# A hybrid decoder layer: other orders of the first two recurrence blocks, SSD rows turned by DMA with a new chunk order, and the FFN's first down rows and third weight rows asked for sooner

## The chip, the cores and the metric

The kernel runs on one core of one Trainium2 chip. The metric is the device time of one execution in microseconds. A core has five engines with a queue of instructions each: TensorE (PE, with its weight loads PEld), VectorE (DVE), ScalarE (ACT), GpSimd (POOL) and SyncE (SP, which issues most of the DMAs here). Each engine takes its own queue in order; engines wait for each other only through semaphores.

## The reference

One decoder layer over 2048 tokens of width 1024, in float32. The first half has two mixers side by side on the normalised rows: a state-space mixer (SSD, 8 heads of 64, chunks of 128 tokens) and an RWKV-7 recurrence (8 heads of 64). Their outputs, side by side, go through one matrix, are normalised and added to the input. The second half is a gated FFN of width 2816 with a causal convolution of 3 taps.

```python
def reference(x, ...):
    xn = _rms_norm(h, pre_mix_norm[l])
    p_ssd, p_rwkv = jnp.split((xn @ w_in[l]).astype(jnp.float32), [SSD_COLS], axis=-1)
    y_ssd = _ssd_mixer(p_ssd, ...)
    y_rwkv = _rwkv7_mixer(p_rwkv, ...)
    mix = jnp.concatenate([y_ssd, y_rwkv], axis=-1).astype(h.dtype) @ w_out[l]
    h = h + _rms_norm(mix, post_mix_norm[l])
    hn = _rms_norm(h, pre_ffn_norm[l])
    u = _causal_dwconv(hn @ ffn_w_up[l], ffn_conv_w[l], ffn_conv_b[l])
    gate, val = jnp.split(u, 2, axis=-1)
    f = (jax.nn.silu(gate) * val) @ ffn_w_down[l]
    h = h + _rms_norm(f, post_ffn_norm[l])
```

## The kernel before

Three phases follow each other on PE, and each begins before the one ahead of it has ended. A matmul operand is kept as two float16 numbers, a rounded one (hi) and the rest (lo), and a product is the sum of three passes over these.

**Phase R, the recurrence** (to about 1005 us): 16 blocks of 128 tokens. The order of the work is written out by hand in strings, one token for a step: FIRST for block 0, SECOND for block 1 (PE still finishes block 0 there), PLAN for those that follow. In FIRST the weights also come in: w.k loads one piece of them and splits it into hi and lo on ACT and DVE. f.d.k and f.conv.k are projections of the block, f.gram.k its Gram matrices gr, from which DVE makes G, which goes through DRAM and comes back as atl; f.chain.k is a quarter of a triangular solve on DVE, 8 steps of a multiplication and an addition on atl and xl. conv makes the convolution of two column groups of the SSD's input: its last part, on ACT, POOL and DVE, makes ca. In phase R's block 0 the order of ACT and DVE is the order of the code; later the framework schedules all engines but PE.

**Phase S, the SSD** (about 950 to 1436 us): 16 chunks of 128 tokens. S_PLAN is the order of one chunk n, of which a letter says which chunk a step serves: c this one, n the next, p the one before, q that of two before, s and t a pair of chunks; Z takes one gate projection (z, 6 matmuls) from a list. p.o.a.b is the product with the output weights, q.post.0 and q.post.1 finish the rows of a chunk: two norms (ACT squares into a spare view, POOL makes the reciprocal roots, DVE scales), the residual on POOL, then the rows xi, ready for the FFN, are turned by PE, four 128 x 128 blocks in each part, copied out of PSUM by ACT into hT (128 x 8 x 128, one buffer) and written to DRAM as HN. hT also serves as the spare view for the squares. S_TAIL is the order behind the last chunk, where F takes one product of the FFN.

**Phase F, the FFN** (from 1378 us): two halves of 1024 tokens, each with 22 rows f of up-products (u, seven of them a row, 12 matmuls each) and 11 pairs of down-products (d). The inner products of both use seven products in place of eight, so operands are sums of blocks made on POOL (us, L1355) and split into hi and lo on ACT (L1224) and DVE or POOL (L1229, L1231). Rows f = 0 and 1 run in code order, as one product per F of S_TAIL. From f = 2 on the steps go to Program: it knows what each reads and writes, gives each a due time from PE's order, and at each moment lets an engine take the ready step with the smallest due time less LEAD, a number for the kind of step ("V C0 C0" is a DVE step that writes C0 from C0).

SP issues the DMAs in the order of the code or of the scheduler, and an issue that waits holds those behind it. The steps of the change are in the class of phase R's blocks (load, conv, chain, from L392), the chunk's post (L1079) with its lines L1085 (square), L1087, L1088, L1093 (xi), L1098 (transposes ht), L1099 (hT), L1101 (HN), and the loop over f in phase F (L1771).

## Time and profile before

| what | value |
| --- | --- |
| time, median of 3 runs | 2658.02 us (2654.33 to 2658.92) |
| the profiled execution | 2655.3 us |
| its span, first to last instruction | 2653.5 us |
| mean granted clock of TensorE | 0.977 of full |
| busy: PE, DVE, ACT, POOL | 93%, 74%, 46%, 47% of the span |
| mean DMA rate | 117 GB/s |

The busy share is an average over stretches with different limits, so the table by stretch, further down, tells more. A line such as "L1098 PE MATMUL ht<-ident_s,xi" names the line of the kernel, the engine, the operation, and the tiles written and read; xN is a count. TensorE's clock has two levels, 2.4 and 1.2 GHz; a mean of 0.98 over a stretch says that it stood at the lower one for 4% of the time.

### The profile page before, as it was taken

How to read it: one execution, taken by the hardware profiler on the slowest of the kernel's cores; microseconds unless marked ns; L12 is line 12 of the kernel's file. 1: busy time of each engine (PE TensorE's matmuls, PEld its weight loads, DVE VectorE, ACT ScalarE, POOL GpSimd, SP SyncE). 2: the span in 40 equal slices, each digit the busy share in tenths (PEclk: the TensorE clock that was granted, in tenths of full speed). 3: DMA queues.
4: the chain of work that ended last, by engine and by line, in shares of the span. 5: the costliest groups of instructions: out<-in, count | busy, mean ns of one | idle time of the engine just before them, and what ended most of it. 6: DMA issues, size and time to landing. Idle time of an engine off the chain costs nothing. (4 is left out here: it accounts for less than half of the span.)

```text
span 2653.5 us, 53912 instructions
## 1 busy us (share of the span) xinstructions
PE 2454.5 (93%) x21324; PEld 1551.8 (58%) x21340; DVE 1951.9 (74%) x3655; ACT 1210.2 (46%) x2467; POOL 1258.0 (47%) x1324
## 2 busy tenths in 40 slices
PE   5889999899999888999998899999989999999998
PEld 4788888888888855555543344444434444444443
DVE  6777777777777765666668879999999836555557
ACT  6555556555555443444444554544453433223132
POOL 2344444444444352333456865867667623123135
PEclk8899999999999998999999999999999999999999
DMA  7233222232222253344355454444435543333243
GB/s 213 71 66 73 54 54 63 61 83 58 54 62 56 49 178 106 124 131 138 126 179 192 132 174 163 137 173 143 171 119 196 182 143 103 100 99 107 84 154 112
DMA packets 309341, 310.74 MB, mean 117 GB/s; under 512 B 168160, under 2 KB 213600, under 8 KB 305760
## 3 DMA queue, kind: packets, MB, share of 16 engines
q1 hardware_dynamic: 307792, 305.72, 38.2%
q8 instruction: 167, 2.74, 0.4%
q10 hardware_dynamic: 1296, 1.58, 0.2%
q14 instruction: 86, 0.70, 0.1%
HBM read 187.85 MB, written 110.99 MB: 113 GB/s over the span
## 5 line engine op out<-in xcount | busy, mean ns | idle before, releaser
L1383 PE MATMUL u<-b,w 128*128 128x512 f16 x3696 | 810.8, 382 | 18.1 <-DVE C L1401 7.1
L1383 PEld LDWEIGHTS <-w 128*128 128x128 f16 x3696 | 362.7, 98 | 462.6 <-issue 25.9
L294 PE MATMUL d<-xt,wr 128*128 128x129 f16 x5376 | 338.1, 225 | 17.8 <-DMA xt<-xh 15.5
L294 PEld LDWEIGHTS <-wr 128*128 128x128 f16 x5376 | 323.9, 101 | 31.8 <-ACT wr L257 15.5
L1619 PE MATMUL d<-dw,fa 128*128 128x512 f16 x1512 | 332.1, 379 | 4.8 <-DMA dw<-DW 2.5
L1619 PEld LDWEIGHTS <-fa 128*128 128x128 f16 x1596 | 156.2, 98 | 203.8 <-issue 15.5
L1401 DVE TENSOR_TENSOR C<-u,C 128x512 f32<-128x512 f32 x220 | 150.5, 685 | 160.6 <-PE u L1383 155.5
L294 PE MATMUL c<-xt,wc 128*128 128x131 f16 x3072 | 204.0, 227 | 21.7 <-ACT tv L434 10.6
L294 PEld LDWEIGHTS <-wc 128*128 128x128 f16 x3072 | 188.2, 100 | 36.0 <-issue 29.5
L1632 DVE TENSOR_TENSOR acc<-d,acc 128x512 f32<-128x512 f32 x212 | 140.1, 683 | 52.1 <-PE d L1619 51.2
L581 DVE TENSOR_TENSOR tmp<-atl,xl 128x60 f32<-128x60 f32 (+24 forms) x465 | 136.4, 293 | 48.4 <-DMA atl<-ATd 33.0
L1229 POOL TENSOR_TENSOR fa<-p,fa 128x512 f16<-128x512 f32 x100 | 142.7, 1441 | 41.5 <-ACT fa L1224 41.5
L1231 DVE SCALAR_TENSOR_TENSOR w<-us,w 128x512 f16<-128x512 f32 x132 | 143.1, 1094 | 24.7 <-ACT w L1224 23.1
L1436 DVE SCALAR_TENSOR_TENSOR p<-C,fpar,p 128x1024 f32<-128x1024 f32 x88 | 129.4, 1470 | 34.1 <-ACT p L1432 34.0
L457 DVE SCALAR_TENSOR_TENSOR ca<-rc,cw,ca 128x128 f32<-128x128 f32 x384 | 132.7, 391 | 21.8 <-POOL ca L452 21.5
L584 DVE TENSOR_TENSOR xl<-xl,tmp 128x60 f32<-128x60 f32 (+24 forms) x465 | 127.9, 275 | 11.2
L1397 ACT ACTIVATE C<-u 128x512 f32<-128x512 f32 x88 | 52.3, 594 | 176.4 <-PE u L1383 157.8
L1436 DVE SCALAR_TENSOR_TENSOR a<-C,fpar,a 128x1024 f32<-128x1024 f32 x88 | 125.6, 1427 | 4.1 <-ACT a L1432 2.3
L1355 POOL TENSOR_TENSOR us<-us,us 128x512 f32<-128x512 f32 x66 | 105.5, 1602 | 48.6 <-DVE w L1231 31.0
L1224 ACT ACTIVATE fa<-p 128x512 f16<-128x512 f32 x110 | 65.6, 624 | 131.0 <-DVE p L1449 118.1
L1224 ACT ACTIVATE w<-us 128x512 f16<-128x512 f32 x132 | 80.7, 623 | 86.5 <-POOL us L1355 51.1
L694 POOL TENSOR_TENSOR tS<-S,Pi 64x256 f32<-64x256 f32 x64 | 40.5, 633 | 167.5 <-DVE S L704 165.1
...
## 6 DMA issues: line engine op xcount, KB each, us to landing
...
```

The costliest lines, as they stand in the source:

```text
L294: nc.tensor.matmul(ps, w[:, a, kt, :], xt[:, b, kt, cols], start=n == 0, stop=n == 3 * KT - 1)
L457: V.scalar_tensor_tensor(out=acc[:, q], in0=raw[:, q, k:k + 128], scalar=cw[:, g + q, k:k + 1], in1=acc[:, q], op0=ALU.mult, op1=ALU.add)
L581: chain.tensor_tensor(out=tmp[:, :m, :n], in0=atl[:, j, j + 1:32].unsqueeze(1).to_broadcast([P, m, n]), in1=xl[:, :m, j:j + 1].to_broadcas ...
L584: chain.tensor_tensor(out=xl[:, :m, j + 1:32], in0=xl[:, :m, j + 1:32], in1=tmp[:, :m, :n], op=ALU.add)
L1224: S.activation(h, src, AF.Copy, **({} if scale is None else {"scale": scale}))
L1229: {"V": V, "G": G_}[engine].tensor_tensor(out=l, in0=src, in1=h, op=ALU.subtract)
L1231: V.scalar_tensor_tensor(out=l, in0=src, scalar=scale, in1=h, op0=ALU.mult, op1=ALU.subtract)
L1383: nc.tensor.matmul(bk[at], self.w[i][:, u, k, :], self.half.b[i][:, k, v, :], start=start and n == 0, stop=n == 11, skip_group_check=True)
L1401: op("V", .61, lambda: V.tensor_tensor(out=part(j, x), in0=bk[at], in1=part(*a), op=ALU.add), (("u", 4 * s + at), (*(c0, c1)[a[0]], a[1])) ...
L1436: V.scalar_tensor_tensor(out=o[j], in0=C[j][:, 2 - d:1026 - d], scalar=cw[:, g, 2 - d:3 - d], in1=o[j], op0=ALU.mult, op1=ALU.add)
L1619: nc.tensor.matmul(bk[s, t], pairs[m].a[i][:, u, t * P:t * P + P], pairs[m].w[n][0][:, v, :], start=new and m == 0 and u == v == 0, stop=m ...
L1632: V.tensor_tensor(out=acc[j][:, t], in0=bk[s, t], in1=acc[j][:, t], op=ALU.add)
```

## The change

Four things change. (1) The numbers of LEAD. (2) The orders FIRST and SECOND; for them conv can leave out its last part, which becomes a step of its own (taps), and the chain comes in eight parts of four steps and not four of eight. (3) In phase S the rows xi are turned by DMA: ACT rounds 512 columns to float16 (hl), DVE puts the rest in xi's own place, SP issues a DMA transpose of each (128 x 512 into 128 x 4 x 128, tile tu, one buffer), POOL adds the two into hT, and HN is written in two parts; PE and PSUM have no share in it. S_PLAN and S_TAIL have new orders. (4) The pools of the first down rows are opened, and the rows asked for, ahead of f = 1; the weights of f = 2 are asked for behind the fourth product of f = 1, and not behind the last.

```diff
@@ -59,7 +59,7 @@
 
-    LEAD = {"A C0 u": 21, "A p p": 20, "A w us": 23, "G cy C1": 36, "G fa fa": 6, "G rt r": -38, "Q r -": -4, "Q us -": -40, "V C0 C0": 27, "V C1 C0": 9, "V C1 C1": 1, "V a1 C1": 7, "V acc acc": -4, "V b b": 3, "V dw dw": 2, "V hx acc": 11, "V p C0": 8, "V p a1": -2, "V p p": 7, "V w p": 16, "V w us": -4}
+    LEAD = {"A C0 u": 16, "A fss acc": 9, "A p p": 12, "A w us": 20, "G cy C1": 40, "G rt r": -38, "Q r -": -4, "V C0 C0": 40, "V C1 C0": 10, "V C1 C1": 1, "V a1 C1": 9, "V acc acc": -4, "V b b": 3, "V hx acc": 9, "V p C0": 9, "V p a1": -2, "V p p": 7, "V w p": 12, "V w us": -4}
@@ -180,33 +180,40 @@
 S_RIGHT = (
-    "ident_s mhalf_s", "ssm pov por ss pnv pnr", "Y", "yr", "xi", "m", "gpost", "gpre2", "hT", "yt", "wo",
+    "ident_s mhalf_s", "ssm pov por ss pnv pnr", "Y", "yr", "xi", "m", "gpost", "gpre2", "hT", "hl", "tu", "yt", "wo",
 )
...
+F_SOON = (*(f"fa{i}0" for i in range(7)), "r0", "rt0")
 F_LATE = (
-    *(f"fa{i}{s}" for i in range(7) for s in range(2)), "acc0", "acc1", "acc2", "acc3", "acc4", "r0", "r1", "rt0", "rt1",
-    "dw", "fss fs2 fov for",
+    *(f"fa{i}1" for i in range(7)), "acc0", "acc1", "acc2", "acc3", "acc4", "r1", "rt1", "dw", "fss fs2 fov for",
 )
...
 S_PLAN = """
-c.begin c.decay.0 Z c.off p.norm c.keys Z c.decay.1 p.o.0.0 Z t.sums s.steps p.o.0.1 t.flip Z n.rows q.post.0 c.y c.state
-p.o.1.0 q.post.1 p.o.1.1
+c.begin Z c.off c.decay.0 Z p.norm Z Z c.decay.1 p.o.0.0 p.o.0.1 c.keys t.sums q.post.0 s.steps q.post.1 c.y t.flip
+n.rows p.o.1.0 c.state p.o.1.1
 """
 S_QUOTA = (3,) * 12 + (4,) * 3
 S_TAIL = """
-F F p.o.0.0 p.norm F p.o.0.1 p.o.1.0 p.o.1.1 F q.post.0 F q.post.1 F F F F F F p.post.0 F p.post.1
+F F F p.norm F F p.o.0.0 p.o.0.1 q.post.0 F p.o.1.0 F p.o.1.1 F q.post.1 F F p.post.0 F p.post.1 F
 """
 FIRST = """
...
+f.solve.1 f.chain.0 f.d.11 f.conv.0 f.chain.1 n.load f.conv.1.0 f.chain.2 f.taps.1 f.conv.2 f.d.12 f.chain.3 w.20
...
 """
 SECOND = """
...
+f.d.0 b.values f.d.1 f.d.2 f.d.3 f.d.4 f.low.0 b.own.0 f.low.1 f.scan f.d.5 f.keys f.d.6 f.d.7 f.d.8 b.merge.0 f.d.9
...
 """
@@ -436,7 +443,7 @@
-            def conv(self, g):
+            def conv(self, g, post=1):
 
                 i, q = self.it, g % 2
                 if q == 0:
@@ -444,9 +451,14 @@
                 dense(tc, self.pc[:, q, 0:131], WC[:, g], self.xt, slice(13, 144))
                 if q == 0:
                     return
-                g -= 1
-                raw = wk.tile([P, 2, 131], F32, name=f"rc_{i}_{g}", tag="raw", bufs=2)
-                S.activation(raw, self.pc[:, :, 0:131], AF.Copy)
+                self.rc = wk.tile([P, 2, 131], F32, name=f"rc_{i}_{g}", tag="raw", bufs=2)
+                S.activation(self.rc, self.pc[:, :, 0:131], AF.Copy)
+                if post:
+                    self.taps(g)
+
+            def taps(self, g):
+
+                i, raw, g = self.it, self.rc, g - 1
                 acc = wk.tile([P, 2, P], F32, name=f"ca_{i}_{g}", tag="ca", bufs=2)
                 for q in range(2):
                     G_.tensor_scalar(
@@ -570,20 +582,20 @@
                 if not begin:
-                    for k in range(4):
+                    for k in range(8):
                         self.chain(k)
 
             def chain(self, part):
                 atl, xl, tmp, XTd, it = self.atl, self.xl, self.tmp, self.XTd, self.it
                 chain = G_ if it == iters - 1 else V
-                for j in range(part * 8, min(part * 8 + 8, 31)):
+                for j in range(part * 4, min(part * 4 + 4, 31)):
                     n, m = 31 - j, j // 4 + 1
                     chain.tensor_tensor(
                         out=tmp[:, :m, :n], in0=atl[:, j, j + 1:32].unsqueeze(1).to_broadcast([P, m, n]),
                         in1=xl[:, :m, j:j + 1].to_broadcast([P, m, n]), op=ALU.mult)
                     chain.tensor_tensor(
                         out=xl[:, :m, j + 1:32], in0=xl[:, :m, j + 1:32], in1=tmp[:, :m, :n], op=ALU.add)
-                if part < 3:
+                if part < 7:
                     return
                 for q in range(4):
                     nc.sync.dma_start(
@@ -1080,8 +1092,8 @@
             if part == 0:
                 ss = wk.tile([P, 1], F32, name="ssm" + self.cf, tag="ssm")
-                self.hT = wk.tile([P, KT, P], F32, name="hT" + self.cf, tag="hT")
-                jk = self.hT.rearrange("p a b -> p (a b)")[:, 0:D // 2].bitcast(BF16)
+                self.hl = wk.tile([P, D], F16, name="hl" + self.cf, tag="hl")
+                jk = self.hl.bitcast(BF16)
                 S.activation(jk, m, AF.Square, accum_out=ss)
@@ -1092,13 +1104,17 @@
-            ps = (bank(f"ht{self.cf}{part}", "yb") if n >= N - 2 else bank(f"ht{self.cf}{part}", "o", 2))
-            for u in range(4):
-                kt = 4 * part + u
-                nc.tensor.transpose(ps[:, u, :], self.xin[:, kt * P:(kt + 1) * P], K.ident)
-            S.activation(self.hT[:, 4 * part:4 * part + 4, :], ps, AF.Copy)
-            if part == 1:
-                nc.sync.dma_start(HN[n // 8][:, :, P * (n % 8):P * (n % 8) + P], self.hT)
+            cs = slice(512 * part, 512 * part + 512)
+            hi = self.hl[:, cs]
+            S.activation(hi, self.xin[:, cs], AF.Copy)
+            lo = self.xin[:, 512 * part:512 * part + 256].bitcast(F16)
+            V.tensor_tensor(out=lo, in0=self.xin[:, cs], in1=hi, op=ALU.subtract)
+            tu = wk.tile([P, 2, 4, P], F16, name=f"tu{self.cf}{part}", tag="tu")
+            nc.sync.dma_start_transpose(tu[:, 0], hi)
+            nc.sync.dma_start_transpose(tu[:, 1], lo)
+            hT = wk.tile([P, 4, P], F32, name=f"hT{self.cf}{part}", tag="hT")
+            G_.tensor_tensor(out=hT, in0=tu[:, 0], in1=tu[:, 1], op=ALU.add)
+            nc.sync.dma_start(HN[n // 8][:, 4 * part:4 * part + 4, P * (n % 8):P * (n % 8) + P], hT)
 
@@ -1770,16 +1786,21 @@
             ready = []
             for f in range(NFF):
                 u = ups[n * NFF + f]
-                for _ in u.run():
+                if n == 0 and f == 1:
+                    ctx.enter_context(wk.open("left", F_SOON))
+                    pairs[0].load()
+                for k, _ in enumerate(u.run()):
                     if n == 0 and f < 2:
                         yield
+                        if f == 1 and k == 3:
+                            ups[2].weights()
                 if n == 0 and f < 2:
                     yield
                 if n == 0 and f == 1:
                     ctx.enter_context(wk.open("left", F_LATE))
                     ctx.enter_context(psp.open("left", [f"u{i}" for i in range(4, 8)]))
                     acc.extend(wk.tile([P, 4, Q], F32, name=f"acc{j}") for j in range(5))
-                if f < NFF - 1:
+                if f < NFF - 1 and (n, f) != (0, 1):
                     ups[n * NFF + f + 1].weights()
                 if fin and f < 4:
                     for j in (2 * f, 2 * f + 1):
@@ -1790,7 +1811,8 @@
                 if f % 2:
                     p = pairs[f // 2]
                     p.factors(ups[n * NFF + f - 1], u)
-                    p.load()
+                    if (n, f) != (0, 1):
+                        p.load()
                     ready.append(p)
                 if n == 0 and f == 1:
                     prog.on = True
```

SP, in the middle of the SSD, before; H, yr, xi and HN are rows written, the recurrence's output read, the input's rows read and the turned rows written, R and rows the decay's rows, xbc and xs the SSD's inputs:

```order
L1089 DMA H4_87<-m_4_19061 128x1024
L1062 DMA yr_6_19526<-YR3_76 128x8x128
L1064 DMA xi_5_19271<-in_x_dram 128x1024
L1101 DMA HN0_81<-hT_4_19369 1024x1x128
L869 DMA xbc_5_19662<-XC5_70 128x2048
L1089 DMA H5_88<-m_5_19273 128x1024
L929 DMA rows_4_19576<-pp_4_19570 16x384
L984 DMA R_8_19578<-rows_4_19576 3x8x128
L984 DMA R_9_19835<-rows_4_19576 3x8x128
L1062 DMA yr_7_19733<-YR3_76 128x8x128
L1064 DMA xi_6_19528<-in_x_dram 128x1024
L1101 DMA HN0_81<-hT_5_19581 1024x1x128
```

SP at the same place after:

```order
L1101 DMA H4_87<-m_4_19077 128x1024
L1113 DMA_TRANSPOSE tu_40_19343<-hl_4_19325 128x4x128
L1114 DMA_TRANSPOSE tu_40_19343<-xi_4_19075 128x4x128
L1117 DMA HN0_81<-hT_40_19346 128x4x128
L1113 DMA_TRANSPOSE tu_41_19411<-hl_4_19325 128x4x128
L1114 DMA_TRANSPOSE tu_41_19411<-xi_4_19075 128x4x128
L1074 DMA yr_6_19549<-YR3_76 128x8x128
L1076 DMA xi_5_19290<-in_x_dram 128x1024
L1117 DMA HN0_81<-hT_41_19414 128x4x128
L1101 DMA H5_88<-m_5_19292 128x1024
L1113 DMA_TRANSPOSE tu_50_19609<-hl_5_19591 128x4x128
L1114 DMA_TRANSPOSE tu_50_19609<-xi_5_19290 128x4x128
```

One HN becomes two, each behind a pair of transposes, and the transposes of the second half stand behind the first half's HN; L1113 reads the rounded half, L1114 the rest.

POOL in the middle of the SSD before, from the root of chunk 4's first norm (pov, por) to chunk 5's; m is the chunk's row, yt and ST the SSD's output and state, sgv and sgr the root for the norm of y:

```order
L1016 TENSOR_TENSOR yt_6_19204<-yt_6_19204,of_6_19233 128x512
L1088 TENSOR_TENSOR m_4_19061<-m_4_19061,xi_4_19059 128x1024
L1040 TENSOR_TENSOR ST1_17148<-ST0_17147,aend_6_19196 128x512
L272 TENSOR_SCALAR pnv_19380<-ssh_4_19378 128x1
L273 TENSOR_TENSOR pnr_19381<-pnv_19380,mhalf_s_18043 128x1
L272 TENSOR_SCALAR sgv_19406<-sgs_6_19402 128x2
L273 TENSOR_TENSOR sgr_19407<-sgv_19406,mhalf_s_18043 128x2
L272 TENSOR_SCALAR pov_19583<-ssm_5_19580 128x1
L273 TENSOR_TENSOR por_19584<-pov_19583,mhalf_s_18043 128x1
```

POOL at the same place after, from behind chunk 4's por:

```order
L1028 TENSOR_TENSOR yt_6_19222<-yt_6_19222,of_6_19241 128x512
L279 TENSOR_SCALAR pnv_19336<-ssh_4_19334 128x1
L280 TENSOR_TENSOR pnr_19337<-pnv_19336,mhalf_s_18049 128x1
L1052 TENSOR_TENSOR ST1_17148<-ST0_17147,aend_6_19214 128x512
L1116 TENSOR_TENSOR hT_40_19346<-tu_40_19343 128x512
L279 TENSOR_SCALAR sgv_19432<-sgs_6_19428 128x2
L280 TENSOR_TENSOR sgr_19433<-sgv_19432,mhalf_s_18049 128x2
L1116 TENSOR_TENSOR hT_41_19414<-tu_41_19411 128x512
L279 TENSOR_SCALAR pov_19593<-ssm_5_19590 128x1
L280 TENSOR_TENSOR por_19594<-pov_19593,mhalf_s_18049 128x1
```

Two additions (L1116) that read what the transposes wrote stand in the row now, one ahead of the y norm's root and one ahead of the next chunk's pov.

DVE in block 0 of the recurrence before, from the first half of G; wr and wc are weights split from wst, and xl and tmp the chain's tiles:

```order
L550 TENSOR_TENSOR G_0_268<-gr00_0_701,cst_195 128x512
L550 TENSOR_TENSOR G_0_268<-gr01_0_702,cst_195 128x512
L258 SCALAR_TENSOR_TENSOR wr_204<-wst13_713,gwr_237,wr_204 128x4x128 x2
L258 SCALAR_TENSOR_TENSOR wc_205<-wst14_719,gwr_237,wc_205 128x4x128 x2
L258 SCALAR_TENSOR_TENSOR wc_205<-wst15_725,gwr_237,wc_205 128x4x128 x2
L258 SCALAR_TENSOR_TENSOR wc_205<-wst16_731,gwr_237,wc_205 128x4x128 x2
L550 TENSOR_TENSOR G_0_268<-gr10_0_737,cst_195 128x512
L550 TENSOR_TENSOR G_0_268<-gr11_0_738,cst_195 128x512
L258 SCALAR_TENSOR_TENSOR wc_205<-wst17_763,gwr_237,wc_205 128x4x128 x2
L258 SCALAR_TENSOR_TENSOR wc_205<-wst18_819,gwr_237,wc_205 128x4x128 x2
L258 SCALAR_TENSOR_TENSOR wc_205<-wst19_825,gwr_237,wc_205 128x4x128 x2
L399 COPY xt_1_831<-xt_0_239 128x16x3
L581 TENSOR_TENSOR tmp_0_761<-atl_0_755,xl_0_760 128x31
```

DVE at the same place after:

```order
L562 TENSOR_TENSOR G_0_268<-gr00_0_707,cst_195 128x512
L562 TENSOR_TENSOR G_0_268<-gr01_0_708,cst_195 128x512
L265 SCALAR_TENSOR_TENSOR wc_205<-wst14_719,gwr_237,wc_205 128x4x128 x2
L265 SCALAR_TENSOR_TENSOR wc_205<-wst15_750,gwr_237,wc_205 128x4x128 x2
L562 TENSOR_TENSOR G_0_268<-gr10_0_756,cst_195 128x512
L562 TENSOR_TENSOR G_0_268<-gr11_0_757,cst_195 128x512
L265 SCALAR_TENSOR_TENSOR wc_205<-wst16_768,gwr_237,wc_205 128x4x128 x2
L265 SCALAR_TENSOR_TENSOR wc_205<-wst17_774,gwr_237,wc_205 128x4x128 x2
L265 SCALAR_TENSOR_TENSOR wc_205<-wst18_780,gwr_237,wc_205 128x4x128 x2
L265 SCALAR_TENSOR_TENSOR wc_205<-wst19_786,gwr_237,wc_205 128x4x128 x2
L593 TENSOR_TENSOR tmp_0_804<-atl_0_798,xl_0_803 128x31
```

Two rows of weight splits now stand between the halves of G where there were four, and four stand between the second half and the chain where there were three and a copy.

## Rows read from the trace of the kernel before

**Rows 1.** The page's busy times: us, share of the span and instructions of an engine.

```profile
PE 2454.5 (93%) x21324; PEld 1551.8 (58%) x21340; DVE 1951.9 (74%) x3655; ACT 1210.2 (46%) x2467; POOL 1258.0 (47%) x1324
```

**Rows 2.** The table by stretch: the window, its length, then busy us (and instructions) of PE, PEld, DVE, ACT and POOL, TensorE's granted clock, the DMA share and GB/s.

```profile
15.53:94.84 79.31, 50.45 (x587) 46.46 (x588) 60.47 (x140) 44.23 (x89) 19.89 (x20) 0.76 0.57 165
94.84:150.00 55.16, 53.30 (x896) 49.78 (x893) 37.46 (x108) 31.28 (x73) 20.95 (x27) 1.00 0.28 64
...
1039.10:1378.40 339.30, 319.22 (x1833) 183.28 (x1846) 226.60 (x405) 152.66 (x414) 133.80 (x149) 0.98 0.40 130
1378.40:1506.20 127.80, 110.92 (x489) 49.51 (x488) 101.30 (x96) 60.57 (x96) 94.56 (x76) 0.93 0.52 170
1506.20:1960.00 453.80, 446.85 (x2065) 201.49 (x2064) 415.60 (x447) 217.10 (x332) 316.97 (x241) 1.00 0.46 158
1960.00:2000.00 40.00, 29.89 (x115) 12.29 (x115) 37.05 (x44) 17.80 (x27) 14.66 (x12) 0.87 0.37 119
2000.00:2590.00 590.00, 584.96 (x2708) 264.38 (x2708) 361.99 (x417) 182.03 (x264) 209.92 (x231) 1.00 0.42 130
```

**Rows 3.** PE's waits for xi from 1039.1 to 1378.4 (us in total, times, longest), and the group of the transposes in the same stretch (busy us, mean ns, idle before).

```profile
PE ht L1098 <- DVE xi L1093: 11.8, 11, 3.1
...
L1098 PE MATMUL ht<-ident_s,xi 128*128 128x128 f32 x112 | 17.5, 279 | 12.0 <-DVE xi L1093 11.8
```

**Rows 4.** PE's timeline in one chunk: start, us, engine, line, operation; from one chunk's psc to the next's, with the second group of transposes and what follows it.

```profile
1084.43 0.61 PE L973 MATMUL psc<-xbc 128*128 128x128 f32 x4
...
1104.05 0.60 PE L1098 MATMUL ht<-ident_s,xi 128*128 128x128 f32 x4
1104.49 2.75 PE L1073 MATMUL o<-wo,Y 128*128 128x512 f16 x12
...
1107.52 0.61 PE L973 MATMUL psc<-xbc 128*128 128x128 f32 x4
```

**Rows 5.** The timelines of ACT, DVE and POOL in the same chunk: the square of the first norm, xi, and the y norm's root.

```profile
1087.81 1.06 ACT L1085 ACTIVATE hT<-m 128x1024 bf16<-128x1024 f32 x1 [1.06 <-DMA HN<-hT]
...
1096.98 1.28 DVE L1093 SCALAR_TENSOR_TENSOR xi<-m,pnr,gpre 128x1024 f32<-128x1024 f32 x1 [1.84 <-POOL pnr L273]
...
1104.02 0.22 POOL L272 TENSOR_SCALAR sgv<-sgs 128x2 f32<-128x2 f32 x1 [7.07 <-ACT sq L1030]
```

**Rows 6.** Durations of like operations on 512 columns: an ACT copy to float16 (minimum, median, maximum in ns), a DVE and a POOL operation on two tiles (busy us and mean ns, in the SSD), and the issue of HN.

```profile
L1224 ACT ACTIVATE w<-us x132: 611/623/633, 1342.0 to 1956.4; 128x512 f16<-128x512 f32 x132
...
L1056 DVE TENSOR_TENSOR Y<-pY,Y 128x512 f16<-128x512 f32 x14 | 9.5, 678 | 0.0
...
L1016 POOL TENSOR_TENSOR yt<-yt,of 128x512 f32<-128x512 f32 x14 | 18.3, 1306 | 0.0
...
L1101 SPq DMA_DIRECT2D HN<-hT x16: 518/561/571, 1059.4 to 1436.0; - x16
```

**Rows 7.** SP's timeline where a DMA that reads a transpose's result waits for it (XN behind xt; between them one other issue of two), the first transpose of the kernel, PE's wait for it, which ends with its first matmul at 15.53, and two small DMAs of the SSD of which the second reads what the first wrote (12 KB).

```profile
71.48 1.23 SPq L405 DMA_TRANSPOSE xt<-xin  x1
72.77 1.16 SPq L371 DMA_DIRECT2D wst<-in_w_c_dram  x2
74.57 0.54 SPq L406 DMA_DIRECT2D XN<-xt  x1
...
11.14 1.37 SPq L404 DMA_TRANSPOSE xt<-xh  x1
...
PE d L294 <- DMA xt<-xh: 15.5, 1, 15.5
...
1076.27 0.33 SPq L929 DMA_DIRECT2D rows<-pp  x1
1077.67 0.60 SPq L984 DMA_DIRECT2D R<-rows  x2
```

**Rows 8.** PE's waits from 1378.4 to 1506.5: us in total, times, longest.

```profile
PE ht L1098 <- DVE xi L1093: 5.6, 1, 5.6
PE u L1383 <- ACT w L1224: 5.1, 1, 5.1
PE u L1383 <- DVE C L1401: 2.4, 1, 2.4
PE ht L1098 <- ACT hT L1099: 2.3, 1, 2.3
```

**Rows 9.** The timelines of DVE, ACT and PE in block 0 of the recurrence; in brackets the idle time before and what ended it.

```profile
55.05 1.41 DVE L258 SCALAR_TENSOR_TENSOR wr<-wst,gwr,wr 128x512 f16<-128x512 f32 x2
56.37 4.06 DVE L258 SCALAR_TENSOR_TENSOR wc<-wst,gwr,wc 128x512 f16<-128x512 f32 x6
60.35 1.28 DVE L550 TENSOR_TENSOR G<-gr,cst 128x512 f32<-128x512 f32 x2
...
69.25 0.19 DVE L581 TENSOR_TENSOR tmp<-atl,xl 128x31 f32<-128x31 f32 x1 [3.07 <-DMA atl<-ATd]
...
80.64 0.42 ACT L461 ACTIVATE ct<-ca 128x256 f32<-128x256 f32 x1 [11.12 <-DVE ca L457]
...
83.12 2.80 PE L294 MATMUL c<-xt,wc 128*128 128x131 f16 x24 [10.62 <-ACT tv L434]
```

**Rows 10.** PE's two largest waits after 1506.5: us in total, times, longest.

```profile
PE d L1619 <- DVE dwx L1583: 6.0, 3, 3.5
PE u L1383 <- ACT C L1397: 4.9, 1, 4.9
```

More of the change, by code (lines that the diff above doesn't have):

```diff
@@ L202 @@
 S_TAIL = """
-F F p.o.0.0 p.norm F p.o.0.1 p.o.1.0 p.o.1.1 F q.post.0 F q.post.1 F F F F F F p.post.0 F p.post.1
+F F F p.norm F F p.o.0.0 p.o.0.1 q.post.0 F p.o.1.0 F p.o.1.1 F q.post.1 F F p.post.0 F p.post.1 F
 """
 FIRST = """
-w.0 w.1 w.2 w.3 f.d.0 w.4 w.5 l. f.d.1 f.d.2 f.low.0 f.d.3 w.6 f.low.1 f.d.4 f.d.5 w.7 w.8 f.keys f.scan w.9 w.10 f.norm f.d.6 w.11 f.d.7 f.d.8 f.d.9 f.receptance w.12 f.gram.0 w.13 w.14 w.15 w.16 f.gram.1 f.solve.1 w.17 f.d.10 f.conv.0 w.18 w.19 n.load f.chain.0 f.chain.1 f.conv.1 f.chain.2 w.20 f.d.11 f.d.12 f.d.13 w.21 f.conv.2 f.transposed.0 f.conv.3 f.conv.4 f.conv.5 f.transposed.1 f.conv.6 f.chain.3 f.conv.7
+w.0 w.1 l. w.2 w.3 w.4 w.5 f.d.0 f.d.1 f.low.0 f.d.2 f.d.3 f.d.4 w.6 f.low.1 w.7 f.d.5 f.scan w.8 f.keys w.9 w.10
+f.norm f.d.6 f.d.7 w.11 w.12 f.d.8 f.d.9 f.receptance w.13 f.gram.0 w.14 f.d.10 w.15 f.gram.1 w.16 w.17 w.18 w.19
+f.solve.1 f.chain.0 f.d.11 f.conv.0 f.chain.1 n.load f.conv.1.0 f.chain.2 f.taps.1 f.conv.2 f.d.12 f.chain.3 w.20
+f.conv.3.0 f.transposed.0 w.21 f.conv.4 f.chain.4 f.chain.5 f.transposed.1 f.d.13 f.taps.3 f.conv.5.0 f.conv.6
+f.chain.6 f.taps.5 f.chain.7 f.conv.7.0 f.taps.7
 """
 SECOND = """
-f.d.0 b.values f.d.1 f.d.2 f.low.0 f.d.3 f.d.4 f.low.1 f.scan f.d.5 f.d.6 f.d.7 b.own.0 f.d.8 f.conv.0 b.merge.0 f.keys f.d.9 f.conv.1 f.norm f.conv.2 f.conv.3 b.merge.1 f.conv.4 b.update.0 f.receptance f.gram.0 f.conv.5 f.gram.1 b.state.0 f.conv.6 f.conv.7 b.own.1 f.solve b.update.1 f.d.10 n.load f.d.11 f.d.12 b.gate f.transposed.0 b.state.1 b.finish.0 f.transposed.1 f.d.13
+f.d.0 b.values f.d.1 f.d.2 f.d.3 f.d.4 f.low.0 b.own.0 f.low.1 f.scan f.d.5 f.keys f.d.6 f.d.7 f.d.8 b.merge.0 f.d.9
+f.conv.0 f.conv.1 f.norm f.conv.2 f.conv.3 b.merge.1 f.receptance f.conv.4 b.update.0 f.gram.0 f.conv.5 f.gram.1
+f.d.10 f.conv.6 f.conv.7 b.state.0 b.own.1 f.d.11 b.update.1 f.transposed.0 b.gate f.solve f.transposed.1 f.d.12
+b.state.1 b.finish.0 f.d.13 n.load
 """
```

## The prediction

> **What bounds the kernel now.** I read the page's busy times first [rows 1]: PE is busy 2454.5 of 2653.5 us, so 199 us are idle, and no edit can give more than those, plus what PE loses where its granted clock falls. Then the table by stretch [rows 2], to see where the 199 lie. The reader is to see four kinds of stretch: the start of the recurrence (15.53 to 94.84), PE 50.45 of 79.31 us at clock 0.76; the SSD chunks (1039.10 to 1378.40), PE 319.22 of 339.30, clock 0.98; the seam into the FFN (1378.40 to 1506.20), PE 110.92 of 127.80, clock 0.93; and the FFN after it, 446.85 of 453.80 and 584.96 of 590.00, which has nothing to give except near 1960. The change touches all four. For each I then read what PE waits for [rows 3, 8, 9, 10], and in the SSD the timeline of one chunk [rows 4, 5]. The chain of waits from the end was of no use here: it is PE for most of its length.
>
> **SSD rows turned by DMA.** Before, PE turns the rows of one chunk in two groups of four transposes; the instruction behind a group starts 0.44 us after it (1104.05 to 1104.49) [rows 4]. The stretch has 112 transposes, 28 groups [rows 3]: 28 x 0.44 = 12.3 us of PE. In front of them PE waits 11.8 us for xi, in 11 places [rows 3]. Both go, since the new step has no PE instruction: 24.1 us. The clock of 0.98 over 339.30 us is work lost for 0.02 x 339.3 = 6.8 us; it falls only where PE waits, so it may go too, which makes 30.9 us the most. What stays is a chunk of 23.09 us (1084.43 to 1107.52 by its psc rows) [rows 4] less 0.88 and less 11.8/14 = 0.84: 21.4 us.
>
> The question is whether the new way keeps up with 21.4 us. It is a loop through one buffer: hl is written by the square of the next chunk, and may be only when the DMA transposes of this one have read it. Its steps: from the square at 1087.81 to the end of xi at 1096.98 + 1.28 = 10.45 us [rows 5]; ACT's rounded half 0.62, DVE's rest 0.68 [rows 6]; the transposes of the first half landing; POOL's add 1.31 and the issue of HN 0.56 [rows 6], behind which SP holds the second half's two transposes; these issued, and landed. No row shows a transpose of 512 columns. From above: one of 1024 columns issues in 1.23 us, and SP, idle at 73.93, goes on at 74.57, 3.09 us after it began; at the start, where two stand back to back among weight loads, the first has landed after 15.53 - 11.14 = 4.39 [rows 7]. From below: 12 KB written at 1076.27 are ready by 1077.67, 1.40 us, and a plain issue costs 0.33 [rows 7]. I take half the issue, 0.62, and 2.3 for the landing, between 1.40 and 3.09. The loop is then 10.45 + 0.62 + 0.68 + 2.3 + 1.31 + 0.56 + 0.62 + 2.3 = 18.8 us, under 21.4: PE sets the pace. With 1.23 and 3.09 it is 10.45 + 0.62 + 1.23 + 3.09 + 1.31 + 0.56 + 1.23 + 3.09 = 21.6; with 4.39 twice 24.2.
>
> What else is added per chunk has cover: ACT does two copies of 0.62 in place of its two copies of hT; DVE gets 2 x 0.68, and was busy 226.60 of 339.30; POOL gets 2 x 1.31, busy 133.80; SP up to four more issues of 1.23, and holds seven short ones. POOL's first add stands ahead of the y norm's sgv, so sgv waits for the DMA as well; sgv started at 1104.02 [rows 5], what follows it is wanted by PE in the next chunk's pY, after 1108, so some 3 us are to spare. Without that cover each us late would be a us of PE per chunk. The chunk's new order moves bc behind z products and the two first halves of o together; the rest of PE's idle time there (339.30 - 319.22 - 11.8 = 8.3) I let stand, and set 2 us against waits that no row shows. SSD: 24.1 - 2 = 22 us off, with the ends -31 and, at a loop of 24.2, 14 x (24.2 - 23.1) = +15 us.
>
> One rule of the Trainium skill speaks against this edit. The Trainium skill, VectorE: DVE Perf Modes, section "The three transpose paths" and the table of rules, gives 390 ns to TensorE and 1309 ns to the DMA for one 128 x 128 block of 2-byte numbers, and sends it to TensorE where PSUM will do as a destination. The row shows one instruction of eight such blocks issued in 1.23 us and landed within 3.09 [rows 7], so the trace bears out that figure of the Trainium skill as a price of an instruction and not of each block. Charged by the block, half a row would take 4 x 1.309 = 5.2 us (an estimate from that page of the Trainium skill), the loop 10.45 + 0.62 + 0.62 + 5.2 + 1.31 + 0.56 + 0.62 + 5.2 = 24.6, and the SSD would grow by 14 x 1.5 = 21 us.
>
> **The tail of the SSD and the first FFN rows.** Of 127.8 us PE waits 16.9: 5.6 and 2.3 at transposes, which go; 5.1 for a weight split on ACT, 2.4 for C [rows 8]. Four transpose groups go, 4 x 0.44 = 1.8. The clock of 0.93 costs 0.07 x 127.8 = 8.9 [rows 2], which follows those waits. So 7.9 + 1.8 = 9.7 at least leave PE, but DVE is busy 101.30 of the 127.80 [rows 2]; what PE gains it may lose again at the next wait on w or C, which DVE and ACT feed. The third weight rows and first down rows are asked for earlier: those queue on SP, and are wanted here at 1468 and 1506. I take 10 off: as much as the transposes held, the rest of the clock against the returning wait. Ends: -3, if the wait for w at 1468 only grows; -22, with every wait but 5 us gone.
>
> **The first recurrence blocks.** PE stands 10.62 us at 83.12 for tv, which ACT gives late, since ACT waited 11.12 us for ca, which DVE takes up only behind the chain's first two quarters, begun at 69.25 after 3.07 us for atl [rows 9]. atl goes out behind the second half of G, which DVE does at 60.35 behind six weight splits of 4.06 us. The new order puts four splits between the halves (in pairs of 0.68, 4.06/6 each) and not eight (1.41 + 4.06): 8 x 0.68 to 4 x 0.68, 2.7 us less, of which one pair's 1.36 comes back behind it; and eight short chain parts let tv's steps in between. The last two weight rows (w.20, w.21) still come late, so PE will wait for those instead: most of the 10.62 stays. I take 5 off, with 0 and -8 as ends; the second order has 1.86 us of idle in 94.84 to 150 to win [rows 2], and I take nothing for it.
>
> **The planner's numbers.** They alter which of ready steps an engine takes in the FFN. PE's own order there is the same, and PE is 99% busy, so the only stretch with something to win or lose is 1960 to 2000, 29.89 of 40 us busy [rows 2], with a wait of 4.9 for C and 6.0 for dwx [rows 10]. I count 0, and 6 to either side.
>
> **The sum.** -22 - 10 - 5 + 0 = -37. The profiled execution took 2655.3 us, which is 1.8 over its span and 2.7 below the median 2658.02. So 2655.3 - 37 = 2618.3, and against the median 2621.
>
> **Rivals.**
> 1. The loop through hl sets the pace without being slower than now (landing near 3.1 us at full issue cost, plus a us at SP): 21.6 + 0.9 = 22.5, so 14 x 0.6 = 8 us less in the SSD, 8 + 10 + 5 = 23 in all: about 2635. For it: SP takes its queue in order, and HN's issue waits on POOL in front of the second transposes. Against it: half the bytes.
> 2. The loop is slower than the old chunk (23.09 us). Place: the SP queue, second transposes behind HN; price 14 us for each us of excess; it decides once the excess passes 15/14 = 1.1 us, when it eats what tail and start give: a landing of about 4.3 us. At 4.39 it is +15 - 15 = 0, 2658; with one more issue of 1.23 ahead in SP's queue the loop is 25.4, +32 - 15: 2675. For it: the 4.39 us row, and the DMA share of 0.40 here [rows 2]. Against it: that row lies among the loads of the start, at DMA share 0.57.
>    By the block price of the Trainium skill (VectorE: DVE Perf Modes, above) this case would come true.
> 3. All waits and the clock come back: 31 + 22 + 8 = 61 less, 2597. Against it: a wait on another engine mostly takes the place of the one removed.
> 4. The FFN's new order costs: steps for C (V C0 C0 goes from a lead of 27 to 40) taken first make weights or down rows late, say 0.7 us in each of the 42 rows behind the first two, 29 us of the 37: about 2650. Against it: PE is idle there only 6.95 + 10.11 + 5.04 = 22 us in 1084 [rows 2].
> 5. The change does not do what it says, in part: the early load of the first down rows takes DMA and SP from the SSD's tail, and the seam gives nothing: 2631, inside the range.
>
> **How the numbers follow.** The forecast with its own ends (rival 5 in it), 2608 to 2635: 0.55. Rival 1: 0.17. Rival 2: 0.12. Rival 3: 0.07. Rival 4: 0.09. For 8 times in 10 I leave out the upper part of rival 2 and the lower part of rival 3: 2602 to 2656. About 0.2%, 5 us, is what a measurement here can tell from no change, so faster is below 2652.7: forecast, rivals 1, 3 and most of 4, 0.85; same: 0.06, rival 2 near its threshold and the rest of 4; slower: 0.09, rival 2 beyond.
>
> **What would show it.** In the profile after: no PE wait for xi and no ht rows; psc rows 21 to 21.5 us apart (22 or more: rival 1; over 23.1: rival 2, with ACT's square waiting for a DMA of hl). DMA transposes of 512 columns issued in 0.6 us and the next HN about 2.3 + 1.3 us behind. In the seam the first d row 37 us sooner than 1506.20, 10 of these behind the last o. At the start, block 1's first d near 90 and not 94.84. It would be wrong if the SSD chunks do not shrink, or if the FFN between 1506 and 2590, now 98 to 99% busy, shows new waits for C or w.

## The result, and the profile after

The changed kernel took 2631.74 us (median of 5 runs, 2626.14 to 2641.48) where the kernel before took 2654.33 on the same chip: a ratio of 0.9914, interval 0.9888 to 0.9940, so 23 us less. The forecast was 37 less: 2621 us, 11 us too low, with the measured time inside its range of 2602 to 2656. A second set with the same kernel gave 0.9912 (0.9896 to 0.9928).

Where the time went is read from the start of the same step in both traces. The table by stretch after, with the columns of [rows 2]; the four windows of [rows 2] that answer to these are 15.53 to 94.84, 1039.10 to 1378.40, 1378.40 to 1506.20 and 1960 to 2000:

```profile
15.42:91.47 76.05, 48.22 (x586) 43.00 (x587) 59.55 (x137) 44.48 (x90) 17.15 (x20) 0.82 0.58 170
...
1028.40:1347.04 318.64, 301.02 (x1720) 170.12 (x1733) 239.08 (x430) 151.85 (x408) 168.90 (x173) 0.99 0.58 159
1347.04:1478.13 131.09, 111.61 (x473) 47.83 (x472) 108.67 (x104) 62.30 (x101) 101.83 (x84) 0.92 0.58 180
...
1931.40:1971.20 39.80, 29.68 (x115) 12.23 (x115) 37.07 (x44) 17.75 (x27) 14.56 (x12) 0.87 0.37 120
```

The SSD's chunks shrank from 339.30 to 318.64 us: 20.7 less, with PE 18.2 less busy and 2.5 less idle. The seam into the FFN did not shrink but grew, from 127.80 to 131.09, with DVE busy 108.67 and not 101.30, POOL 101.83 and not 94.56. From the first down product to PE's last one nothing moved (1506.20 to 2643.06 before, 1478.13 to 2615.93 after: 1136.9 and 1137.8; the stretch around 1960 is 39.80 for 40.00).

PE's waits in the SSD after, the answer to [rows 3], and in the seam, the answer to [rows 8]; us in total, times, longest:

```profile
PE bc L1003 <- DMA R<-rows: 5.1, 5, 1.6
PE acs L933 <- DVE nac L923: 4.0, 2, 2.3
PE bc L1002 <- ACT aend L1010: 3.2, 2, 1.9
PE px L975 <- DVE ST L1058: 2.6, 2, 1.8
...
PE u L1399 <- DVE C L1417: 7.2, 2, 4.0
PE u L1399 <- DVE b L1245: 5.6, 2, 4.6
PE u L1399 <- ACT w L1240: 3.8, 1, 3.8
PE u L1399 <- ACT b L1240: 1.5, 2, 1.1
PE u L1399 <- ACT C L1413: 0.7, 1, 0.7
PE u L1399 <- DVE w L1247: 0.5, 1, 0.5
```

The waits for xi are gone, 11.8 us, and four others stand there with 14.9 in all. In the seam the two waits at transposes (5.6 and 2.3) are gone too, and in their place PE waits 5.6 + 1.5 us for b, an operand of the first FFN rows, for which it did not wait before, and longer for C.

The new way of a row, in a chunk that answers to [rows 4, 5]: lines from the timelines of PE, SP, POOL and ACT.

```profile
1072.10 0.60 PE L975 MATMUL px<-ident_s,xbc 128*128 128x128 f32 x4
...
1072.11 0.37 SPq L1076 DMA_DIRECT2D xi<-in_x_dram  x1
...
1072.93 1.06 ACT L1097 ACTIVATE hl<-m 128x1024 bf16<-128x1024 f32 x1
...
1077.16 2.35 POOL L1100 TENSOR_TENSOR m<-m,xi 128x1024 f32<-128x1024 f32 x1 [2.17 <-DMA xi<-in_x_dram]
...
1083.65 1.24 SPq L1113 DMA_TRANSPOSE tu<-hl  x1
1085.25 1.19 SPq L1114 DMA_TRANSPOSE tu<-xi  x1
1089.18 0.39 SPq L1117 DMA_DIRECT2D HN<-hT  x1
1089.76 2.02 SPq L1113 DMA_TRANSPOSE tu<-hl  x1
1091.87 1.21 SPq L1114 DMA_TRANSPOSE tu<-xi  x1
1093.18 0.55 SPq L1074 DMA_DIRECT2D yr<-YR  x1
1094.35 0.36 SPq L1076 DMA_DIRECT2D xi<-in_x_dram  x1
...
1088.00 1.16 POOL L1116 TENSOR_TENSOR hT<-tu 128x512 f32<-128x512 f16 x1 [2.27 <-DMA tu<-xi]
1094.50 1.16 POOL L1116 TENSOR_TENSOR hT<-tu 128x512 f32<-128x512 f16 x1 [1.91 <-DMA tu<-xi]
...
1094.48 0.60 PE L975 MATMUL px<-ident_s,xbc 128*128 128x128 f32 x4
...
1095.31 1.06 ACT L1097 ACTIVATE hl<-m 128x1024 bf16<-128x1024 f32 x1
...
1115.34 0.60 PE L975 MATMUL px<-ident_s,xbc 128*128 128x128 f32 x4
...
ACT hl L1097 <- DMA tu<-hl: 0.3, 1, 0.3
```

From the square at 1072.93 to the landing of the last transpose, read from POOL's second add at 1094.50, is 21.6 us; the next square starts at 1095.31, with no wait for the DMA. A transpose of 512 columns holds SP as long as one of 1024 did in [rows 7] (1.2 us), and POOL's add follows the issue of the second one by 2.75 and 2.63 us. A second loop is to be seen that I had not looked for: xi has one buffer, so its next rows (1072.11, 1094.35) are asked for only when the last transpose has read it, and POOL's residual add waits 2.17 us for them. The two issues are 22.2 us apart, and PE's chunk by its px rows is 22.4; that they keep step does not say which sets the pace. Neither loop has a fixed length: the next chunk takes 20.9 us (1094.48 to 1115.34), and in all 14 chunks the square waits for the transposes once, for 0.3 us (the last line, a sum over the chunks).

### The profile page after: what moved, and what is told of

Its sections match the earlier page's. It is cut to its first block, busy times and chain, and to the rows that moved or that the text cites. A ratio compares the mean times of both kernels' runs of the same rounds, so it can differ in the third digit from the quotient of the medians.

```text
span 2626.4 us, 53869 instructions
## 1 busy us (share of the span) xinstructions
PE 2439.2 (93%) x21196; PEld 1536.1 (58%) x21212; DVE 1970.8 (75%) x3687; ACT 1211.5 (46%) x2467; POOL 1301.0 (50%) x1356
## 5 line engine op out<-in xcount | busy, mean ns | idle before, releaser
L1417 DVE TENSOR_TENSOR C<-u,C 128x512 f32<-128x512 f32 x220 | 150.5, 684 | 156.3 <-PE u L1399 151.0
L1452 DVE SCALAR_TENSOR_TENSOR p<-C,fpar,p 128x1024 f32<-128x1024 f32 x88 | 131.1, 1490 | 33.9 <-ACT p L1448 33.7
L1458 POOL COPY fcarry<-C 128x2 f32<-128x2 f32 x88 | 40.5, 461 | 164.7 <-DVE C L1417 164.7
```

The lines of the kernel that those rows point to most:

```text
L1417: op("V", .61, lambda: V.tensor_tensor(out=part(j, x), in0=bk[at], in1=part(*a), op=ALU.add), (("u", 4 * s + at), (*(c0, c1)[a[0]], a[1])) ...
L1452: V.scalar_tensor_tensor(out=o[j], in0=C[j][:, 2 - d:1026 - d], scalar=cw[:, g, 2 - d:3 - d], in1=o[j], op0=ALU.mult, op1=ALU.add)
```

## The experiments

All ratios are against the kernel before, run on the same chip beside them. Two distances are read from the traces: the chunks, from the third chunk's px to the first FFN product (before 339.7), and the seam, from there to the first down product (before 127.8).

**The parts alone.** The recurrence's part, with the rest of the kernel as before:

```diff
-w.0 w.1 w.2 w.3 f.d.0 w.4 w.5 l. f.d.1 ...
+w.0 w.1 l. w.2 w.3 w.4 w.5 f.d.0 f.d.1 ...
-                for j in range(part * 8, min(part * 8 + 8, 31)):
+                for j in range(part * 4, min(part * 4 + 4, 31)):
```

> The kernel before with the recurrence's part alone: new FIRST and SECOND, conv split, chain in eight parts. The trace after has block 3 of the recurrence starting 7.5 us sooner and the first SSD chunk 9.9 us sooner than before. Theory (this part gives those by itself): 8 to 11 us less than the kernel before, and block 3 near 204.3. Rival (part of the 9.9 is the SSD's own, whose first steps run beside the last blocks): block 3 at 204.3 but the first SSD chunk no more than 7.5 us sooner, total 5 to 7 us less.

Measured 2642.45 us, 0.9957 (0.9938 to 0.9976): about 11 us less, chunks 340.5, seam 127.6. Block 3 starts at 204.09 (before 211.82), the first chunk at 960.32 (972.07). But the recurrence's own time spreads: three other kernels that leave it as it was have block 3 at 207.6 to 209.8. Over all traces block 3 starts 8.5 us sooner than in the profiled run before with the new orders (10 traces) and 2.4 with the old (4, itself among them): some 6 us belong to this part up to there, and 8.5 up to the third chunk.

The SSD's part alone, then its two halves: turning with the old orders, and the new orders with PE turning.

```diff
-            ps = (bank(f"ht{self.cf}{part}", "yb") if n >= N - 2 else bank(f"ht{self.cf}{part}", "o", 2))
+            nc.sync.dma_start_transpose(tu[:, 0], hi)
+            nc.sync.dma_start_transpose(tu[:, 1], lo)
...
-c.begin c.decay.0 Z c.off p.norm c.keys Z c.decay.1 p.o.0.0 Z t.sums s.steps p.o.0.1 t.flip Z n.rows q.post.0 c.y c.state
+c.begin Z c.off c.decay.0 Z p.norm Z Z c.decay.1 p.o.0.0 p.o.0.1 c.keys t.sums q.post.0 s.steps q.post.1 c.y t.flip
```

> The kernel before with the SSD's part alone: rows turned by DMA, new S_PLAN and S_TAIL. Theory (the SSD's 14 chunks give 20.7 us by themselves and the seam loses some 3): 15 to 20 us less than before, the stretch from the third chunk's px to the first FFN product at 319 us and not 339.7. Rival (the seam's loss comes from the earlier loads of down and weight rows, which this kernel does not have): the seam no longer than before, 20 to 23 us less.

Measured 2636.13 us, 0.9930 (0.9907 to 0.9952): 18 less; chunks 322.1, seam 132.1. The theory held, and the rival for the seam fell: the seam loses without any earlier load.

> The kernel before with the rows turned by DMA and the old S_PLAN and S_TAIL. Theory (what gives the SSD's gain is that PE has 28 groups of transposes less, 12.3 us, and no wait for xi, 12 us; order is second): 12 to 24 us less than before. Rival (the old order starts the post late in the chunk, so the loop through hl, tu and SP's queue, 21.6 us by the trace after, bounds the chunk at 23 us or more): 0 to 5 us less, chunks 23 us apart, the square waiting for the transposes.

Measured 2651.91 us, 0.9990 (0.9975 to 1.0005): no difference. The rival's time came, but only in part by its reason: the chunks are 10.6 us shorter (329.2), and the seam is 14.2 longer (142.0), of which one wait of PE for yr, the recurrence's output, is 9.7. The loop is at work in the chunks. These rows show how: one chunk of this kernel in order of time, then two sums over the chunks, and last the wait in the seam:

```profile
1100.54 1.06 ACT L1085 ACTIVATE hl<-m 128x1024 bf16<-128x1024 f32 x1 [2.39 <-DMA tu<-hl]
...
1101.69 1.15 POOL L1104 TENSOR_TENSOR hT<-tu 128x512 f32<-128x512 f16 x1 [3.75 <-DMA tu<-xi]
...
1103.78 1.28 DVE L1087 SCALAR_TENSOR_TENSOR m<-m,por,gpost 128x1024 f32<-128x1024 f32 x1 [3.99 <-POOL por L273]
...
1105.83 0.17 ACT L998 ACTIVATE aend<-bc 128x4 f32<-128x4 f32 x1 [2.36 <-DVE dec L997]
...
1106.06 0.38 PE L990 MATMUL bc<-mnegb,identb 128*128 128x512 bf16 x1 [2.91 <-ACT aend L998]
...
PE bc L990 <- ACT aend L998: 12.4, 12, 2.9
...
ACT hl L1085 <- DMA tu<-hl: 7.8, 5, 2.4
...
PE o L1073 <- DMA yr<-YR: 9.7, 1, 9.7
```

The old order starts a row's finish late in a chunk, and the transposes are still under way when the next square comes. The square waits 2.39 us for them, and POOL's add 3.75, with the root por behind it. DVE's m waits 3.99 for por, the decay's dec (L997) stands behind m on DVE, ACT's aend waits 2.36 for dec, and PE 2.91 for aend. The square waits so in 5 of the 14 chunks; that all of PE's 12.4 us for aend come from this chain is not shown. Why yr comes late in the seam was not tried; its load, on SP, stands behind transposes and the FFN's loads.

> The kernel before with the new S_PLAN and S_TAIL and the rows still turned by PE. Theory (the order by itself gives little, since the transposes with their waits for xi stay on PE): within 6 us of before, PE waits for xi at ht of 10 us or more. Rival (the new order takes away the wait for xi, and the DMA only saves PE's 12 us): 8 to 12 us less than before.

Measured 2642.81 us, 0.9960 (0.9942 to 0.9978): 11 less; chunks 322.9, seam 136.1. My theory fell and the rival held: the order alone takes the wait for xi out of the chunks. But it lengthens the seam by 8.3 us, and there PE waits 12.1 us for xi, 9.7 of it in one place (before 5.6). The chunks of three traces, with the columns of [rows 2], are the recurrence's part alone (old order, PE turning), the new orders alone, and the new orders with DMA turning; last, the wait in the seam of the new orders alone:

```profile
1020.36:1360.90 340.54, 321.61 (x1849) 184.19 (x1848) 226.24 (x405) 152.66 (x414) 133.97 (x148) 0.98 0.40 130
1030.62:1353.47 322.85, 313.56 (x1850) 181.99 (x1849) 213.17 (x404) 152.04 (x409) 132.13 (x147) 0.99 0.43 137
1032.92:1355.06 322.14, 305.47 (x1737) 171.16 (x1736) 242.12 (x431) 152.61 (x409) 170.32 (x174) 0.98 0.57 159
...
PE ht L1098 <- DVE xi L1093: 12.1, 2, 9.7
```

With as many instructions, the orders alone take 8.0 us of busy time from PE in the chunks and 9.6 of idle time (18.9 to 9.3). Turning by DMA takes 8.1 more of busy time, and 7.4 us of idle time come back, so the chunks hardly change. With the new order, turning still adds 0.9960 - 0.9930, some 7 us, and in the traces 454.2 for 459.0 us from the third chunk to the first down product, of which 4.0 are the seam's.

**What holds the seam.** The kernel after without the early asking for down and weight rows, then with the planner's old numbers, then with the old tail.

```diff
-                if n == 0 and f == 1:
-                    ctx.enter_context(wk.open("left", F_SOON))
-                    pairs[0].load()
...
-                        if f == 1 and k == 3:
-                            ups[2].weights()
```

> The kernel after without the early asking: down rows and the weights of the third row where they were. Theory (the seam loses because DVE and POOL are the busy ones there, each DVE step slowed while POOL works, whatever is asked for when): within 3 us of after. Rival (the early loads and the steps they bring push the operand b and the weights of rows 1 and 2 back): 4 to 10 us faster than after, no wait of PE for b.

Measured 2630.78 us, 0.9919 (0.9902 to 0.9936), as after; chunks 322.8, seam 131.1. The early asking costs nothing here and gives nothing that these runs can tell, though the waits in the seam are others: 12.0 us for C at once, 3.9 for b, and none for w on ACT.

```diff
-    LEAD = {"A C0 u": 16, "A fss acc": 9, "A p p": 12, "A w us": 20, ...
+    LEAD = {"A C0 u": 21, "A p p": 20, "A w us": 23, ...
```

> The kernel after with the planner's old numbers. Theory (the numbers only move steps that nobody waits for; PE's order there is the same and the stretch from the seam on is 98 to 99% busy in both): within 3 us of after, all of it between the third row and the first down products. Rival (they were found for the new start and hold it): 4 us slower or more.

Measured 2628.73 us, 0.9913 (0.9898 to 0.9928): the numbers make no difference; chunks 319.7, seam 131.3.

```diff
-F F F p.norm F F p.o.0.0 p.o.0.1 q.post.0 F p.o.1.0 F p.o.1.1 F q.post.1 F F p.post.0 F p.post.1 F
+F F p.o.0.0 p.norm F p.o.0.1 p.o.1.0 p.o.1.1 F q.post.0 F q.post.1 F F F F F F p.post.0 F p.post.1
```

> The kernel after with the old S_TAIL. Theory (in the seam DVE sets the pace, so the order of PE there matters little): within 4 us of after. Rival (the new tail runs the FFN's products too early, before their operand b is there, and loses 6 us by it): 4 to 8 us faster than after, no wait for b of 4.6 us.

Measured 2620.27 us, 0.9888 (0.9870 to 0.9906), which looked like the rival; chunks 318.1, seam 129.3. But in that trace most of the lead was there before the SSD, in a recurrence of the same instructions. So it was run again with the unchanged kernel beside it:

> The kernel after, unchanged, as the control beside the three others. 20 to 26 us less than before. In its trace the stretch from the third chunk's px to the first FFN down product again near 450 us (before 467.5), the seam near 131.

> The kernel after with the old S_TAIL, again. Theory (its lead of some 8 us over the kernel after was mostly the recurrence's own spread between executions, since the trace gives it only 2.8 us in the SSD and the seam): 2 to 5 us faster than the control. Rival (the old tail is worth all of it): 8 us or more faster than the control.

Measured: the control 2627.00 us, 0.9912 (0.9896 to 0.9928), chunks 324.7, seam 131.3; the old tail 2623.41, 0.9911 (0.9890 to 0.9932), chunks 319.6, seam 129.0. No difference in time; the old tail's seam is 2 us shorter in both of its traces. It is not a version that can be called better.

What DVE has to do with the seam was tried by taking work away. This kernel leaves out the lower half of the rows of chunks 14 and 15:

```diff
+            if n < N - 2:
                 V.tensor_tensor(out=lo, in0=self.xin[:, cs], in1=hi, op=ALU.subtract)
...
+            if n < N - 2:
                 nc.sync.dma_start_transpose(tu[:, 1], lo)
```

> The kernel after, with the lower half of the last two chunks' rows left out: no DVE subtraction and no second transpose for chunks 14 and 15, so these rows reach the FFN rounded to float16. Theory (the seam is held by DVE, which got four subtractions of 0.7 to 1.75 us there): the seam 3 to 7 us shorter than in the control, DVE busy some 5 us less in it. Rival (the seam is held by the weights' way from DRAM over POOL and ACT, or by PE's order): the seam within 1.5 us of the control.

Measured 2622.37 us, 0.9897 (0.9880 to 0.9915), which is not clear of the control's; but the seam is 125.96 us, 5.3 shorter than the control's. So the subtractions and their transposes cost that much, as the theory said. They are not all that holds the seam, which without them is still only 1.8 us under the 127.8 of the kernel before. DVE is busy 110.8 us in it, as in the control, so its busy time was the wrong measure. The rows point to the place in its queue. DVE in the seam of the kernel after, then POOL and PE:

```profile
1373.53 1.76 DVE L1247 SCALAR_TENSOR_TENSOR w<-ut,w 128x512 f16<-128x512 f32 x1
1375.22 1.75 DVE L1111 TENSOR_TENSOR xi<-xi,hl 128x512 f16<-128x512 f32 x1
1376.89 1.75 DVE L1247 SCALAR_TENSOR_TENSOR w<-us,w 128x512 f16<-128x512 f32 x1
1378.56 0.68 DVE L1111 TENSOR_TENSOR xi<-xi,hl 128x512 f16<-128x512 f32 x1
1379.16 1.75 DVE L1245 TENSOR_TENSOR b<-hs,b 128x512 f16<-128x512 f32 x1
...
1374.70 3.39 POOL L1371 TENSOR_TENSOR us<-us,us 128x512 f32<-128x512 f32 x2
1378.77 1.59 POOL L1371 TENSOR_TENSOR us<-us,us 128x512 f32<-128x512 f32 x1 [0.68 <-POOL us L1371]
...
1380.96 1.01 PE L1399 MATMUL u<-b,w 128*128 128x512 f16 x2 [4.64 <-DVE b L1245]
```

Two subtractions of a row (L1111) stand ahead of the split of b that PE waits 4.64 us for; with them gone, PE's waits for b on DVE in the seam are 3.2 us in all, and 5.8 in the control. Whether the subtractions or the two transposes that went with them matter more was not tried apart.

**The queue on SP.** R, which bc reads, is issued on SP behind xi's load, and that waits for the last transpose. The kernel after with the pair's sums and flip earlier, so that R goes out ahead of xi:

```diff
-c.begin Z c.off c.decay.0 Z p.norm Z Z c.decay.1 p.o.0.0 p.o.0.1 c.keys t.sums q.post.0 s.steps q.post.1 c.y t.flip
-n.rows p.o.1.0 c.state p.o.1.1
+c.begin Z c.off c.decay.0 Z p.norm Z Z c.decay.1 p.o.0.0 t.sums p.o.0.1 t.flip c.keys q.post.0 n.rows s.steps q.post.1 c.y
+p.o.1.0 c.state p.o.1.1
```

> The kernel after with the pair's sums and flip earlier in S_PLAN and the decay's rows (R) loaded ahead of the input's rows, so that SP does not hold R behind the second half's transposes. Theory (PE in the SSD now waits for what SP's queue holds behind the transposes: 5.1 us for R): that wait goes and the kernel is 3 to 5 us faster. Rival (the loop through hl and tu bounds each chunk at about 21.5 to 22.4 us, so what is gained at R is lost at the next wait): within 2 us of after.

Measured 2637.77 us, 0.9949 (0.9934 to 0.9964): slower than after, chunks 330.7. Neither theory nor rival: the wait for R is gone, but sums now comes while its PSUM bank still holds the decay that ACT reads, and PE waits for that, and for the state:

```profile
PE acs L922 <- ACT aend L1010: 9.8, 6, 2.3
PE px L975 <- DVE ST L1058: 6.9, 4, 2.2
```

Last, two buffers for tu, with the old tail, so that SP need not hold the second half's transposes until POOL has added the first:

```diff
-            tu = wk.tile([P, 2, 4, P], F16, name=f"tu{self.cf}{part}", tag="tu")
+            tu = wk.tile([P, 2, 4, P], F16, name=f"tu{self.cf}{part}", tag="tu", bufs=2)
```

> The kernel after with the old S_TAIL and two buffers for tu, so that SP can issue the second half's transposes without waiting for POOL's add of the first. Theory (the loop through hl, tu and SP's queue still costs a part of each chunk, by the late R and by ACT's and DVE's late steps): 3 to 8 us faster than the kernel with the old S_TAIL, chunks 21 us apart and not 21.3 to 22.4. Rival (PE sets the pace of the chunks since the new order starts the post early): within 2 us of it.

Measured 2627.82 us, 0.9917 (0.9897 to 0.9937): no gain; chunks 319.3, seam 132.9. The theory fell: all four transposes go out together, and R, now behind the last HN, comes later still (PE waits 10.9 us for it, in place of 5.3 and 5.7 with the old tail alone); in the seam PE waits 4.9 us for yr. So taking out the wait for POOL between the transposes gains nothing as it stands; what it or the loop through xi would be worth, were R out of the way, was not tried apart.

## Why the prediction came out as it did

**The SSD, -22: near in size (-20.7 in the trace after, -15.1 in the control's, 15 to 21 less in the five traces with this order and this turning), half right in reason.** I held that 24.1 us leave PE, 12.3 of transposes and 11.8 of waits for xi, because the new step has no PE instruction. The transposes did leave. The waits leave with PE's transposes too, by the order (none is left in the chunks with the orders alone), and in the kernel after 14.9 us of other waits stand there, so PE's idle time fell by 2.5 us only. The "2 us against waits that no row shows" was the term that was too small. What made up for it is busy time, 18.2 us less and not 12.3, and that the two errors nearly cancel is luck. About 8 us of it come with the orders alone, with as many instructions, at a clock of 0.99 for 0.98; the clock, which I had left out of the 22, is worth some 3 of these by those two figures, and it was 0.98 again in the control's chunks. What the rest is stays open. And the order was not "second": 17 us of the chunks' 20.7 come with it alone, 10.6 with the turning alone, which are not to be added.

**The loop, 18.8 us.** Its two sizes were too low: I halved the issue (0.62, measured 1.2) and took 2.3 for a landing (2.6 to 2.8). In the chunk shown the loop is 21.6 us, the value of the sum with full issue and 3.09. It does not set the pace of the kernel after, where the square waits 0.3 us in all and a chunk took 20.9. The 21.4 that I set PE, and the 23.1 at which rival 2 was to begin, came from one chunk of 23.09 us; the mean chunk was 339.30/14 = 24.2 before and is 318.64/14 = 22.8 after. Rival 1's mechanism exists: with the old order the square waits for the transposes, and the chunks give 10.6 us. The new order starts the finish early enough. The Trainium skill (VectorE: DVE Perf Modes, section "The three transpose paths") gives 1309 ns for the DMA's transpose of 128 x 128. Charged by the block, that does not hold here either: four blocks cost SP the same 1.2 us as eight.

**The seam, -10: wrong, it is +3.** This is the step that failed, and it holds most of the error: 13 of the 14 us. I counted the transposes' 9.7 us as leaving PE, and set the clock's 8.9 against the wait that would come back on w or C. The waits at the transposes did leave, but PE's waits for b, w and C grew from 8.3 to 19.3 us, and the clock did not rise (0.92 for 0.93). Two causes are shown. One is the new orders, which I gave no term here: with PE turning they make the seam 8.3 us longer, turning by DMA then takes 4.0 off (132.1), and with the old tail and turning by DMA it is 129.0 to 129.3. The other is DVE. I noted its 101.30 of 127.80 us, but counted what the new step adds on DVE and POOL (2 x 0.68 and 2 x 1.31 a chunk) only where they had cover, in the SSD, and not here, where the last two chunks' rows meet the splits of b and w in DVE's queue: 5.3 us, with the transposes that go with it. How the two share the growth, and what else holds C and w, stays open. Nor is 0.68 the price there. In the trace after, the 7 of the 32 subtractions (L1111) that began while a POOL instruction was running took 1.53 to 1.76 us; the other 25 took 0.68 to 0.69, though POOL began one beside 20 of them. C (L1417), which reads one operand from PSUM, takes 0.68 always (675 to 695 ns over 220 times). The Trainium skill (SBUF — State Buffer, section "Who interferes with whom") has a rule for that: a DVE instruction with two inputs in SBUF contends with a POOL instruction that reads SBUF, and one of the two is held up. The rows agree. POOL's adds of the turned halves (L1116) read SBUF as well.

**The recurrence, -5: right** as far as it can be told: 6 us to block 3, 8.5 to the third chunk, with the start of the chain at 67.48 and not 69.25 us. But not all by the step I named. The 10.62 us wait for tv is gone and two others, 6.9 and 3.0 for rc, stand in its place, as I held for most of it; only 3.4 us are won in block 0. More was won in block 2, 57.85 us for 64.61, clock 1.00 for 0.95, for which I had taken nothing. Over all 14 traces block 0 is 3.0 us shorter, block 1 1.2 longer and block 2 4.5 shorter.

**The planner's numbers, 0: right**, by the run with the old ones. **Rivals.** Rival 1's total of 23 us is the one that came, but not its parts, 8 in the SSD and 10 in the seam; 2 and 4 did not come; 3 came in no part but the clock's in some traces; 5 is what the result looks like (2631 was its price), but not by its reason, since the kernel without the early loads has the same seam.

A last number matters for the sums: the profiled run before was 5.5 us later at the third chunk than the mean of the four traces with the old recurrence, itself among them, so a single pair of traces overstates what the recurrence's part gave.
